# Stacks of q and k formed in place, one store per result of mixer A, and two more pairs of projection tiles by seven half products

## The chip, the cores and the metric

The kernel runs on one core of a Trainium2 chip, in one launch. The metric is the device time of that launch in microseconds (us); lower is better. TensorE (PE) multiplies matrices, VectorE (DVE) and ScalarE (ACT) do elementwise work and move results out of PSUM, GpSimd (POOL) and SyncE (SP) issue DMAs, and POOL also does small copies. Each engine carries out its own instructions in the order in which they stand in the program and waits for the others by semaphores.

## The reference, cut to what matters

One encoder layer for 512 tokens of width 1024, in float32. Two token mixers run beside each other on projections of the input `h`, are gated and merged, and a SwiGLU block follows.

```python
qa, ka, va, qb, kb, vb = jnp.split(h @ w_in, SPLITS, axis=-1)      # 16, 4, 4, 12, 12, 12 heads of 64
qa, ka, qb, kb = (rope_partial(t, pos) for t in (qa, ka, qb, kb))  # rotates the first 16 of 64
o_a = windowed_gqa_sink(qa, ka, va, a_sink)     # |i-j| <= 128, 4 query heads per key head
o_b = dilated_mixture(qb, kb, vb)               # (window, stride) = (128,1), (512,4), (2048,16)
g_a, g_b = jnp.split(jax.nn.sigmoid(h @ w_gate + b_gate), 2, axis=-1)
y = (g_a * (o_a @ w_br_a) + g_b * (o_b @ w_br_b)) @ w_out
h = layer_norm(DN_ALPHA * h + y, ln1_g, ln1_b)
f = (silu(h @ w_ff_gate) * (h @ w_ff_up)) @ w_ff_down
h = layer_norm(DN_ALPHA * h + f, ln2_g, ln2_b)
```

## The kernel before, in words

**Numbers.** Each float32 operand of a matmul is split into a rounded high part and a low part (what the rounding left), and a product is three matmuls: high by high, high by low, low by high. ACT (sometimes DVE) makes the high part, DVE the low part by a subtraction. For attention, high and low parts stand as a *stack* of 128 partitions: for a query head the 64 rows of its high part above the 64 rows of its low part, for a key head the high part twice (`t`) and the low part twice (`kl`), or, for the dilated groups, pairs of high and low columns, twice (`k_pairs`). `q_post`, `k_post` and `k_pairs` form them after the rotation: one copy and one subtraction give the parts of both heads of a tile, and SP's DMAs (`move`, L821; in `k_pairs` L866) put 64 rows at a time in their places.

**Projection tiles.** A tile of 128 output features is a sum over eight blocks of 128 inputs: 24 matmuls of 512 columns (`feat_k`, L533 to L535). Two tiles together can also be formed by `pair_x` (L649 to L651) as a 2 by 2 block product with seven instead of eight half products, 12 matmuls of 256 columns each, so 84 in all. It loads five half-tile weights and adds two more onto them by accumulating DMAs of POOL (L397), forms two sums on DVE, and splits seven half tiles instead of four. ACT and DVE put the results together.

**Attention.** Mixer A has four groups of heads (words `A0` to `A3`), each in four blocks of 128 queries. Mixer B has four head slots (`B0` to `B3`). In B, a block's statistics are exchanged between partition blocks by POOL's small copies (L1128, L1129) ahead of the normalisation. The outputs of A leave in DRAM tiles `oa`, two stores of 64 partitions per block (L1056). Later `fetch_oa` (words `O`) loads two heads as 128 rows (SP, L1317) and adds their other part by an accumulating DMA of POOL (L1318).

**Order.** `ORDER` lists the work in words: `P:x,y` a pair by `pair_x`, `T:x`, `Q..`, `K..` a single tile, `q`, `g`, `V..` further single tiles, `R` the rotation of the tiles gathered so far, `A`, `B`, `O` as above. A planner at build time (`Program.run`) gives each operation a due time from the PE work ahead of it and then fixes the order of every engine by costs that stand in the code. It also hands out the SBUF slots. Raw weight halves are limited by `ws` (`N_WS` = 6), split ones by `whl` (`N_WHL` = 12, two slots per half), later somewhat more (`ROOMS`). After the mixers come the branch products, `w_out`, the feed-forward block (also with seven half products) and the last layer norm; the change edits nothing there.

Of the kernel before, what the change touches and what calls it, by code (L numbers as in the profile page):

```python
# [9 lines left out]
F32 = mybir.dt.float32  # L10
# [5 lines left out]
P = 128  # L16
# [36 lines left out]
SPARE, SPARE2 = 12, 12  # L53
# [12 lines left out]
RATE, RATE2, ACC = 1.4, 1.3, 290  # L66

# [19 lines left out]
VA q1 A0 q2 q3 g X P:k1,q4 R A1 P:q5,g P:q6,q7 R A2 P:g,g A3 P:g,g L P:Q00,K00 R V12 P:Q01,K01 R P:Q02,K02 R V0 B0 Q10 K10 R Q11 K11 R B1 O O Q12 K12 R O O B2 B3 O O O O g8  # L87
"""
FORMS = -60.0
VAL = -100.0  # L90
OA_AFTER = (0, 0, 0, 0, 0, 0, 0, 0)
# [3 lines left out]
BY_DMA = ()  # L95
AWAY = range(8, 16)
N_WSA, N_WHLA = 8, 16
# [36 lines left out]
class Program:  # L134
# [68 lines left out]
    def run(self):  # L203
# [27 lines left out]
        while n_left:  # L231
# [13 lines left out]
            while progress:  # L245
                progress = False
                for e in engines:
# [31 lines left out]
                    if e == SP:  # L279
                        end = now + (0.62 if 14 < now < SLOW else 0.47)  # L280
                        moved = max(moved, now + 0.9) + (1.5 if now < 9.5 else RATE if 90 < now < 165 else RATE2 if 285 < now < 325 else 1.0 if now < SLOW else 0.92) * cost
                        o.done = moved + (LATE if 95 < now < 150 else 2.4 if 14 < now < SLOW else 0.87)
                    elif o.moves:
                        end = now + cost
                        moved = max(moved, end + 0.3) + (1.0 if 14 < now < SLOW else 0.92) * o.moves
                        o.done = moved + (0.87 if e == ACT else 6.2 if ACC < now < 420 else 3.2 if 14 < now < SLOW else 2.2)
                    else:
                        end = now + cost
                        o.done = end
# [51 lines left out]
def hybrid_layer(ctx: ExitStack, tc: tile.TileContext, wpack, xT, xtok, sink, bgate,  # L341
# [262 lines left out]
    def pair_x(ua, ub):  # L604
# [12 lines left out]
        def form(key, of, x, y):  # L617
            tt(lambda: W[of].t, lambda: W[x].t, lambda: W[y].t, ALU.add, [W[x], W[y]], [W[of]], S, -LOOK)
            W[key] = W[of]
# [92 lines left out]
    def turn_rows(tiles):  # L712
# [12 lines left out]
        op([(DVE, dve(S, extra=0.03))], lambda e: nc.vector.stream_shuffle(h_(), g(), SHUF2), reads=gs, writes=[H], prio=EV)  # L725
        op([(DVE, dve(S))], lambda e: nc.vector.tensor_tensor(g(), g(), c.t[0:n], op=ALU.mult),
           reads=[*gs, *[(c, i) for i in range(4)]], writes=gs, prio=EV)
        op([(DVE, dve(S))], lambda e: nc.vector.tensor_tensor(h_(), h_(), s_.t[0:n], op=ALU.mult),
           reads=[H, *[(s_, i) for i in range(4)]], writes=[H], prio=EV)
# [78 lines left out]
    def both_parts(ps, nt):  # L808

        R = rotate(ps)  # L810
        x, y = slot(F32R), slot(F32R)
        op(cp_alts(S, cut=CUT), lambda e: copy(e, view(x.t, nt, False), view(R.t, nt, True)),
           reads=[R], writes=[x, (y, "room")], prio=EV)
        op([(DVE, dve(S, extra=CUT))], lambda e: nc.vector.tensor_tensor(
            view(y.t, nt, False), view(R.t, nt, True), view(f32(x.t), nt, False), op=ALU.subtract),
           reads=[R, x], writes=[y], prio=EV)
        return x, y

    def move(dst, d, src, c, key, rooms=()):

        op([(SP, 0.4)], lambda e: nc.sync.dma_start(f32(dst.t[d:d + 64]), f32(src.t[c:c + 64])), reads=[src],  # L821
           writes=[(dst, key), *rooms], prio=EV)

    def q_post(ps, nt, kv_half):

        x, y = both_parts(ps, nt)
        out_ = []
        for a in (0, 64):
            t = slot(F32R)
            move(t, a, x, a, "h", [(t, "room")])  # L830
            move(t, 64 - a, y, a, "l")
            out_.append((t, a))
        return out_

    def k_post(ps, nt):

        x, y = both_parts(ps, nt)
        out_ = []
        for a in (0, 64):
            t, kl = slot(F32R), slot(F32R)  # L840
            for b, src in ((t, x), (kl, y)):
                for d, key in ((a, "h"), (64 - a, "d")):
                    move(b, d, src, a, key, [(kl, "room" + key)] if b is t else [])
            out_.append((t, kl))
        return out_

    def k_pairs(ps):

        R = rotate(ps)
        zs, out_ = [], []  # L850
        for n in range(2):
            z, c = slot(F32R), slice(n * (S // 2), (n + 1) * (S // 2))
            zs.append(z)
# [7 lines left out]
        for a in (0, 64):  # L861
            ts = []
            for z in zs:
                t = slot(F32R)
                for d, key in ((a, "h"), (64 - a, "d")):
                    op([(SP, 0.4)], lambda e, t=t, z=z, a=a, d=d: nc.sync.dma_start(  # L866
                        f32(t.t[d:d + 64]), f32(z.t[a:a + 64])), reads=[(z, "h"), (z, "l")],
                       writes=[(t, key)] + ([(t, "room")] if key == "h" else []), prio=EV)
                ts.append(t)
            out_.append(tuple(ts))  # L870
        return out_
# [14 lines left out]
    def turned_values(u, nt, turn_by=0, done=None):  # L886
# [3 lines left out]
        for i in range(2):  # L890
            ps = done
# [18 lines left out]
        for b in range(NR):  # L910
# [6 lines left out]
            op([(PE, 0.18)], turn, reads=[*src, ident], writes=[pb])  # L917
# [59 lines left out]
    def turned_probs(srcs, toks):  # L977
# [7 lines left out]
        op([(PE, 0.36)], go, reads=[*toks, ident], writes=[pb])  # L985
# [6 lines left out]
    def turned_pairs(srcs, toks):  # L992
# [7 lines left out]
        op([(PE, 0.36)], go, reads=[*toks, ident], writes=[pb])  # L1000
# [12 lines left out]
    oaD = [Buf("dram", None, lambda: dram.tile([2, 4, 64, 4, P], F32, name=name("oa"))) for _ in range(4)]  # L1013
    obT = [slot(F32, "res") for _ in range(2)]

    def unit_a(g, b, qs, kk, vs):
# [38 lines left out]
        for part in range(2):  # L1055
            op([(SP, 0.73)], lambda e, part=part: nc.sync.dma_start(  # L1056
                oaD[g].t[part, :, :, b].rearrange("h p c -> p h c"),
                t.t[64 * part:64 * part + 64].rearrange("p (h c) -> p h c", h=4)), reads=[t], writes=[(oaD[g], b, part)],
               prio=STORE)

    def unit_b(hs, q, k, v0, v1, v2):
# [99 lines left out]
        dil = []  # L1161
        for half in range(2):
# [5 lines left out]
            def pv(e, half=half, xs=xs, od=od):  # L1168
# [7 lines left out]
                y for vs in (v1, v2) for t in vs[2 * half:2 * half + 2] for y in vtok(t)], writes=[od])  # L1176
            t = slot(F32, "att")
            dil.append(t)
            part = lambda od=od: od.t.rearrange("p (r i a) -> p r a i", r=2, a=2)
# [32 lines left out]
        t = slot(F32, "att")  # L1212
        op(cp_alts(S, True), lambda e: copy(e, t.t[0:64], o.t[64:128]), reads=[o], writes=[t])
        a = 64 * (hs % 2)
# [27 lines left out]
    def gate(f, ps=None):  # L1242
        if ps is None:
# [6 lines left out]
           reads=[ps, bg], writes=[t], prio=EV)  # L1250

# [25 lines left out]
    ka = k_near(psk, 4)  # L1277
    qa = q_near(psq, 4, (0, 0))
# [32 lines left out]
    def fetch_oa(k):  # L1311
# [3 lines left out]
        src = lambda part: d.t[part, hs].rearrange("h p b c -> (h p) (b c)")  # L1315
        got = [(d, b, part) for b in range(NR) for part in range(2)]
# [5 lines left out]
    def units_of(w):  # L1322
# [8 lines left out]
        if w[0] == "q":  # L1331
            return U_QA + i, lambda t: qa.extend(q_post(t, 4, ((i // 2) % 2,) * 2))
        if w[0] == "k":
            return U_KA + i, lambda t: ka.extend(k_post(t, 4))
# [4 lines left out]
    def step(w):  # L1339
# [4 lines left out]
        elif w[:2] == "P:":  # L1344
            both = [units_of(x) for x in w[2:].split(",")]
            for (u, f), t in zip(both, pair_x(*[u for u, _ in both])):
# [7 lines left out]
        elif w == "R":  # L1354
            tiles = [t for t, _ in env["turn"]]
            turn_rows(tiles)
# [8 lines left out]
        elif w[0] == "q":  # L1365
            i = int(w[1])
            kv = (i // 2) % 2
            qa.extend(dense_q(U_QA + i, 4, (kv, kv)))
        elif w == "k1":
            ka.extend(dense_k(U_KA + 1, 4))  # L1370
        elif w[0] == "A":
            g = int(w[1])
            for b in range(NR):
                unit_a(g, b, qa[4 * g:4 * g + 4], ka[g], env["va"])
# [4 lines left out]
        elif w[0] in "QK":  # L1379
            pair, g = int(w[1]), int(w[2])  # L1380
            u, f = units_of(w)
            env["turn"].append((in_sbuf(u), f))
        elif w == "V0":
# [11 lines left out]
    for w in ORDER.split():  # L1395
        step(w)

# [167 lines left out]
    def turn_h1(t, j, c0, c1, tok):  # L1565
# [7 lines left out]
        op([(PE, 0.36)], go, reads=[z, ident], writes=[pb], prio=NORM)  # L1573
# [482 lines left out]
```

## Time and profile before

| | |
|---|---|
| median of 3 runs | 727.33 us (727.32 to 727.66) |
| the profiled execution | 727.14 us, its span 725.4 us |
| busy | PE 716.7 us (99%), DVE 655.7 (90%), ACT 472.0 (65%), POOL 133.1 (18%) |
| DMA | 140.30 MB, mean 193 GB/s |

The span runs from the first to the last instruction. Matmuls overlap in their pipeline, so the duration of one matmul is longer than the time from its start to the next one's; the cost of a matmul in a row of matmuls is read from starts.

### The profile page before, as it was taken

The numbers are of one execution on the slowest core, as the hardware profiler recorded it, in microseconds if no ns is written. First come the engines' busy times: TensorE is split into PE (matmuls) and PEld (weight loads), VectorE is DVE, ScalarE is ACT, GpSimd is POOL, SyncE is SP. The second block draws the span as 40 slices with busy tenths as digits, with TensorE's granted clock in tenths as the row PEclk, the third lists the DMA queues.
The fourth block names the chain that finished last, engine by engine and source line by source line (L and its number), as shares of the span: only waits on it lengthen the run. The fifth ranks groups of instructions, "written<-read, shape, count | busy, mean of one in ns | idle before, by whom it ended". The sixth has DMA issues, their size and how long they took to land.

```text
span 725.4 us, 14382 instructions
## 1 busy us (share of the span) xinstructions
PE 716.7 (99%) x4767; PEld 665.7 (92%) x4767; DVE 655.7 (90%) x1408; ACT 472.0 (65%) x1077; POOL 133.1 (18%) x297
## 2 busy tenths in 40 slices
PE   9999999999999999999999999999999999999995
PEld 7889999989998888988888999999999999999985
DVE  6999999889997898898968898899999999899987
ACT  6757798768778665766624666756666566666821
POOL 0021221101100731540020022111112111212000
PEclk9999999999999999999999999999999999999999
DMA  7978788856567699965782499676788878978402
GB/s 250 320 154 199 193 221 245 211 130 173 168 190 188 158 239 249 317 203 163 232 189 71 102 273 239 154 202 148 196 256 215 194 193 246 248 194 195 103 30 87
DMA packets 88010, 140.30 MB, mean 193 GB/s; under 512 B 11136, under 2 KB 24064, under 8 KB 87936
## 3 DMA queue, kind: packets, MB, share of 16 engines
q1 hardware_dynamic: 74336, 114.87, 51.2%
q0 software_dynamic: 13328, 24.39, 20.5%
q8 instruction: 37, 0.61, 0.3%
q14 instruction: 37, 0.30, 0.1%
q10 hardware_dynamic: 272, 0.13, 0.1%
HBM read 114.97 MB, written 7.60 MB: 169 GB/s over the span
## 4 chain that ended last, share of the span: by engine, by line
PE 98%; DMA 1%; DVE 1%; ACT 0%; DVEq 0%; SPq 0%; issue 0%
PE ps L1702 10%; PE ps L1701 9%; PE ps L1700 9%; PE ps L534 9%; PE ps L533 9%; PE ps L535 9%; PE ps L1911 4%; PE ps L1913 4%; PE ps L1912 4%; PE ps L651 3%; PE ps L650 3%; PE ps L649 3%; PE ps L983 3%; PE ps L1491 3%; PE ps L1492 3%; PE ps L1490 3%
## 5 line engine op out<-in xcount | busy, mean ns | idle before, releaser
L383 ACT ACTIVATE sl<-sl 128x512 fp32r<-128x512 f32 (+3 forms) x419 | 231.3, 583 | 58.9 <-DVE sl L554 31.0
L554 DVE TENSOR_TENSOR sl<-sl,sl 128x512 fp32r<-128x512 f32 (+3 forms) x378 | 222.8, 623 | 4.4 <-ACT sl L383 3.4
L383 ACT ACTIVATE sl<-ps 128x256 f32<-128x256 f32 (+5 forms) x209 | 88.5, 445 | 90.9 <-PE ps L1702 56.2
L397 POOL DMA_DIRECT2D sl<-wpack x60 | 53.0, 887 | 341.5 <-DMA sl<-wpack 130.2
L1701 PE MATMUL ps<-sl,sl 128*128 128x256 f32 x352 | 96.8, 275 | 0.0
L1702 PE MATMUL ps<-sl,sl 128*128 128x256 f32 x352 | 96.8, 275 | 0.0
L1700 PE MATMUL ps<-sl,sl 128*128 128x256 f32 x352 | 96.8, 275 | 0.0
L533 PE MATMUL ps<-x,sl 128*128 128x512 f32 (+1 forms) x241 | 93.4, 388 | 0.0
L535 PE MATMUL ps<-x,sl 128*128 128x512 f32 (+1 forms) x241 | 91.3, 379 | 0.0
L534 PE MATMUL ps<-x,sl 128*128 128x512 f32 (+1 forms) x209 | 79.2, 379 | 0.1
L1700 PE MATMUL ps<-x,sl 128*128 128x256 f32 x264 | 72.6, 275 | 0.0
L1701 PE MATMUL ps<-x,sl 128*128 128x256 f32 x264 | 72.6, 275 | 0.0
L1702 PE MATMUL ps<-x,sl 128*128 128x256 f32 x264 | 72.6, 275 | 0.0
L1701 PEld LDWEIGHTS ps<-sl,sl 128*128 128x128 f32 x352 | 67.6, 192 | 0.1
L1700 PEld LDWEIGHTS ps<-sl,sl 128*128 128x128 f32 x352 | 67.6, 192 | 0.1
L1702 PEld LDWEIGHTS ps<-sl,sl 128*128 128x128 f32 x352 | 67.6, 192 | 0.0
L409 DVE TENSOR_TENSOR sl<-sl,sl 128x512 fp32r<-128x512 f32 x94 | 62.9, 683 | 0.8 <-ACT sl L383 0.7
L535 PEld LDWEIGHTS ps<-x,sl 128*128 128x128 f32 x241 | 45.7, 190 | 6.4
L1700 PEld LDWEIGHTS ps<-x,sl 128*128 128x128 f32 x264 | 50.6, 192 | 0.4
L1701 PEld LDWEIGHTS ps<-x,sl 128*128 128x128 f32 x264 | 50.6, 192 | 0.4
L533 PEld LDWEIGHTS ps<-x,sl 128*128 128x128 f32 x241 | 45.8, 190 | 5.6 <-ACT x L383 0.4
L554 DVE TENSOR_TENSOR sl<-sl,ps 128x512 f32<-128x512 f32 (+1 forms) x67 | 44.1, 660 | 7.4 <-PE ps L1913 5.4
(172 smaller groups left out, 1856.9 us busy)
## 6 DMA issues: line engine op xcount, KB each, us to landing
sl<-wpack SPq DMA_DIRECT2D x249, 256.0 KB, 4.0
sl<-wpack POOLq DMA_DIRECT2D x60, 256.0 KB, 5.4
sl<-sl SPq DMA_DIRECT2D x110, 128.0 KB, 3.3
wf<-wpack SPq DMA_DIRECT2D x51, 256.0 KB, 5.4
wf<-wpack POOLq DMA_DIRECT2D x24, 256.0 KB, 5.4
oa<-sl SPq DMA_DIRECT2D x32, 128.0 KB, 3.3
sl<-sl SPq DMA_DIRECT2D x68, 32.0 KB, 2.6
sl<-oa SPq DMA_DIRECT2D x8, 256.0 KB, 4.7
```

Of the source, the lines that this page charges most:

```text
L383: nc.scalar.activation(dst, src, AF.Copy)
L397: op([(POOL, 1.0)], lambda e: nc.gpsimd.dma_start(b.t, src2, accum_op=ALU.add), reads=[b], writes=[b], prio=prio, moves=1.65)
L409: op([(DVE, dve(S))], lambda e: nc.vector.tensor_tensor(l.t, src.t, f32(h.t), op=ALU.subtract), reads=[src, h], writes=[l], prio=prio, abs ...
L533: mm(o, a, x0, start=(k == 0 and begins), stop=False, skip_group_check=split)
L534: mm(o, a, x1, start=False, stop=False, skip_group_check=split)
L535: mm(o, b, x0, start=False, stop=(k == nk - 1), skip_group_check=split)
L554: op([(DVE, dve(w))], lambda e: nc.vector.tensor_tensor(dst(), x(), y(), op=o), reads=reads, writes=writes, prio=prio)
L1700: mm(o, wh, pairs(bh[k]()), start=(first and k == 0), stop=False, skip_group_check=True)
L1701: mm(o, wh, pairs(bl[k]()), start=False, stop=False, skip_group_check=True)
L1702: mm(o, wl, pairs(bh[k]()), start=False, stop=(k == 3), skip_group_check=True)
L1911: mm(ps.t, x0, pairs(w[0].t), start=(first and m == 0), stop=False, skip_group_check=True)
L1912: mm(ps.t, x0, pairs(w[1].t), start=False, stop=False, skip_group_check=True)
```

## The change

Three things are edited, and the planner's constants and the word list with them.

1. `q_post` copies the rounded parts into both stacks at full height, and one move for each head puts the low part over the half that the head doesn't need. `k_post` and `k_pairs` do the same: full copies on ACT, then moves of 64 rows within the tile. A query tile takes 2 moves instead of 4, a key tile 4 instead of 8. Each move now also waits for those who still read the half that it overwrites.
2. The DRAM tiles `oa` are laid out head by head, then part, so a block of mixer A leaves by one store of 128 partitions. A fetch of two heads then reads two runs of 64 rows that don't adjoin, instead of one run of 128 rows.
3. The word list has ten `P:` words instead of eight (`Q10` and `K11`, and one more pair of gates), in another order, and each word may carry a shift of its due time (`@`). All gates with f >= 8 are put away in DRAM and fetched back, three more than before.

```diff
-VA q1 A0 q2 q3 g X P:k1,q4 R A1 P:q5,g P:q6,q7 R A2 P:g,g A3 P:g,g L P:Q00,K00 R V12 P:Q01,K01 R P:Q02,K02 R V0 B0 Q10 K10 R Q11 K11 R B1 O O Q12 K12 R O O B2 B3 O O O O g8
+X@2 g@-35 q1@-105 q2@-149 T:q3@-22 VA@-123 P:k1,q4@-23 R@-465 A0@-87 P:Q00,g@-38 A1@-79 P:q6,q7@-7 P:g,g@-8 R@-25 P:g,g A3@-83 L@-49
+P:q5,K00@-17 R@2 V12@-14 A2 P:Q01,K01@-52 R@-13 P:Q02,K02@-16 R@-62 V0@-6 Q11@-75 P:K11,Q10@-8 R@16 K10@-18 R@-1160 B0@-95 Q12@-15 K12@-37
+g@-17 B1@-63 R@-429 O@-43 O@93 O@-87 B2@-368 g@6 B3@20 O@-46 O@182 O@-16 P:g,g@-4 g@-28 g@2 g O@66 O@85 g@-6
...
     def q_post(ps, nt, kv_half):
-        x, y = both_parts(ps, nt)
-        out_ = []
-        for a in (0, 64):
-            t = slot(F32R)
-            move(t, a, x, a, "h", [(t, "room")])
-            move(t, 64 - a, y, a, "l")
-            out_.append((t, a))
-        return out_
+        R = rotate(ps)
+        q0, q1, l = slot(F32R), slot(F32R), slot(F32R)
+        rounded(R, q0, nt, [(l, "room")])
+        low_of(R, q0, l, nt)
+        move(q0, 64, l, 0, "l", [(q0, "h"), (l, "h")])
+        rounded(R, q1, nt, by_act=True)
+        move(q1, 0, l, 64, "l", [(q1, "h"), (l, "h")])
+        return [(q0, 0), (q1, 64)]
+    def spread(t, u, reads):
+        op(cp_alts(S)[:1], lambda e: copy(e, u.t, f32(t.t)), reads=reads, writes=[(u, "h"), (u, "room")], prio=EV)
     def k_post(ps, nt):
...
+        R = rotate(ps)
+        t0, l0, t1, l1 = [slot(F32R) for _ in range(4)]
+        rounded(R, t0, nt, [(l0, "room")])
+        low_of(R, t0, l0, nt)
+        move(t0, 64, t0, 0, "d", [(t0, "h"), (l0, "h")])
+        rounded(R, t1, nt, [(l1, "room")], True)
+        spread(l0, l1, [(l0, "h")])
+        move(l0, 64, l0, 0, "d", [(l0, "h"), (l1, "h")])
+        move(t1, 0, t1, 64, "d", [(t1, "h")])
+        move(l1, 0, l1, 64, "d", [(l1, "h")])
...
-    oaD = [Buf("dram", None, lambda: dram.tile([2, 4, 64, 4, P], F32, name=name("oa"))) for _ in range(4)]
+    oaD = [Buf("dram", None, lambda: dram.tile([4, 2, 64, 4, P], F32, name=name("oa"))) for _ in range(4)]
...
-        for part in range(2):
-            op([(SP, 0.73)], lambda e, part=part: nc.sync.dma_start(
-                oaD[g].t[part, :, :, b].rearrange("h p c -> p h c"),
-                t.t[64 * part:64 * part + 64].rearrange("p (h c) -> p h c", h=4)), reads=[t], writes=[(oaD[g], b, part)],
-               prio=STORE)
+        op([(SP, 1.46)], lambda e: nc.sync.dma_start(
+            oaD[g].t[:, :, :, b].rearrange("h a p c -> (a p) h c"), t.t.rearrange("p (h c) -> p h c", h=4)),
+           reads=[t], writes=[(oaD[g], b)], prio=STORE)
...
-        src = lambda part: d.t[part, hs].rearrange("h p b c -> (h p) (b c)")
+        src = lambda part: d.t[hs, part].rearrange("h p b c -> h p (b c)")
         op([(SP, 0.73)], lambda e: nc.sync.dma_start(st.t, src(0)), reads=got, writes=[st], prio=OAP[k // 4], after=env["B", OA_AFTER[k]])
         op([(POOL, 1.0)], lambda e: nc.gpsimd.dma_start(st.t, src(1), accum_op=ALU.add), reads=[*got, st], writes=[st],
            prio=OAP[2 + k // 4], moves=1.65)
...
     def gate(f, ps=None):
...
+        if f in AWAY:
+            put_away(f)
...
+LONG = 1.3
```

Three places of the program show what moved; line numbers are those of each kernel's own file.

PE before, at the single tile of `Q10` in the middle of the mixers (`x` are the tokens' high and low parts, `ident` marks a transpose):

```order
L1049 MATMUL ps_3155<-sl_3143,sl_566 128x512
L1050 MATMUL ps_3155<-sl_3144,sl_566 128x512
L533 MATMUL ps_3171<-x_94,sl_2909 128x512
L534 MATMUL ps_3171<-x_103,sl_2909 128x512
L535 MATMUL ps_3171<-x_94,sl_2910 128x512
L915 MATMUL ps_3179<-ident,sl_3045 128x128
```

PE after, where the pair of `K11` and `Q10` begins:

```order
L1018 MATMUL ps_3368<-ident,sl_3179 128x128
L1018 MATMUL ps_3368<-ident,sl_3182 128x128
L659 MATMUL ps_3375<-x_98,sl_3189 128x256
L660 MATMUL ps_3375<-x_105,sl_3189 128x256
L661 MATMUL ps_3375<-x_98,sl_3190 128x256
```

Triples of 512 columns have become triples of 256: over the whole program there are 96 matmuls of 128x512 fewer and 168 of 128x256 more; all others are as many as before, and there is one run of transposes less (50 instead of 51).

SP before, at the first fetches of `oa` (L391 are weights, L722 and L733 rows of the rotation):

```order
L391 DMA sl_3871<-wpack 128x512
L722 DMA sl_3840<-sl_3853 16x512
L1317 DMA sl_3903<-oa_1071 128x512
L1317 DMA sl_3915<-oa_1071 128x512
L391 DMA sl_3921<-wpack 128x512
L733 DMA sl_3573<-sl_3582 16x512 x2
L733 DMA sl_3648<-sl_3582 16x512 x2
L1317 DMA sl_3979<-oa_2048 128x512
L391 DMA sl_3989<-wpack 128x512
```

SP after, at the same place (L842 are the moves within a stack):

```order
L395 DMA sl_3764<-wpack 128x512
L754 DMA sl_3601<-sl_3607 16x512 x2
L732 DMA sl_3507<-sl_3812 16x512 x2
L1369 DMA sl_3846<-oa_1974 128x1x512
L1369 DMA sl_3855<-oa_1021 128x1x512
L1369 DMA sl_3861<-oa_1974 128x1x512
L1369 DMA sl_3877<-oa_3163 128x1x512
L395 DMA sl_3880<-wpack 128x512
L395 DMA sl_3931<-wpack 128x512
L842 DMA sl_3923<-sl_3923 64x512
L842 DMA sl_3919<-sl_3919 64x512
```

Four fetches stand in a row, three more and one follow 21 and 45 rows later; their shape has become one of two runs; SP has 528 transfers instead of 586, 54 moves and 16 stores fewer.

POOL before, behind the copies of a unit of mixer B:

```order
L1128 COPY st_3646<-st_3646 32x2
L1129 COPY st_3646<-st_3646 32x2
L1318 DMA sl_3903<-oa_1071 128x512
L1318 DMA sl_3915<-oa_1071 128x512
L1318 DMA sl_3979<-oa_2048 128x512
L1318 DMA sl_3996<-oa_2048 128x512
L1318 DMA sl_4186<-oa_2534 128x512
```

POOL after, within the copies of a unit of mixer B (`B1`):

```order
L1162 COPY st_3660<-st_3660 32x2
L1370 DMA sl_3846<-oa_1974 128x1x512
L1370 DMA sl_3855<-oa_1021 128x1x512
L1370 DMA sl_3861<-oa_1974 128x1x512
L1370 DMA sl_3877<-oa_3163 128x1x512
L1161 COPY st_3660<-st_3660 32x2
L1162 COPY st_3660<-st_3660 32x2
```

Four accumulating fetches now stand ahead of the last eight copies of `B1`; before they stood behind the last copy.

More of the change, by code (lines that the diff above doesn't have):

```diff
@@ L819, in move, with low_of @@
[L819 to L824, printed above, removed]
-        x, y = both_parts(ps, nt)
-        out_ = []
-        for a in (0, 64):
-            t = slot(F32R)
-            move(t, a, x, a, "h", [(t, "room")])
-            move(t, 64 - a, y, a, "l")
-            out_.append((t, a))
-        return out_
-    def k_post(ps, nt):
[L837 to L845, printed above, removed]
+    def low_of(R, h, l, nt):
+        op([(DVE, dve(S, extra=CUT))], lambda e: nc.vector.tensor_tensor(
+            view(l.t, nt, False), view(R.t, nt, True), view(f32(h.t), nt, False), op=ALU.subtract),
+           reads=[R, (h, "h")], writes=[(l, "h")], prio=EV)
@@ L860, in k_pairs @@
                prio=EV)
[L861 to L871, printed above, removed]
+            zs.append(z)
+        for z in zs:
+            u = slot(F32R)
+            spread(z, u, [(z, "h"), (z, "l")])
+            us.append(u)
+            move(z, 64, z, 0, "d", [(z, "h"), (z, "l"), (u, "h")])
+            move(u, 0, u, 64, "d", [(u, "h")])
+        return [tuple(zs), tuple(us)]
     def scores(o_of, q, qc, k, kc, n):
```

129 lines of the change are left out of this document (89 added, 40 removed).

## The prediction, as it stood before the changed kernel ran

> **What bounds the kernel now.** I read the page first, then TensorE's own waits, then its starts in the timeline, then the stretch of the mixers, where the change lies.
>
> ```profile
> span 725.4 us, 14382 instructions
> ...
> PE 716.7 (99%) x4767; PEld 665.7 (92%) x4767; DVE 655.7 (90%) x1408; ACT 472.0 (65%) x1077; POOL 133.1 (18%) x297
> ...
> PE 98%; DMA 1%; DVE 1%; ACT 0%; DVEq 0%; SPq 0%; issue 0%
> ```
>
> The second line is busy time and share, the last the chain that ended last. A busy TensorE may still wait inside its pipeline, so its waits (waited for: us in total, times, longest) and its end come next:
>
> ```profile
> PE ps L469 <- DVE eps L520: 1.2, 1, 1.2
> ```
>
> ```profile
> 717.62 0.38 PE L1492 MATMUL ps<-sl,sl 128*128 128x512 f32 x1
> 718.04 0.70 DVE L1529 BATCH_NORM_STATS2 st<-ps 128x6 f32<-128x512 f32 x1 [0.68 <-PE ps L1492]
> ...
> 720.53 1.54 DVE L1553 SCALAR_TENSOR_TENSOR sl<-sl,st,sl 128x512 f32<-128x512 f32 x3
> ```
>
> TensorE waits once, 1.2 us at the start. Its last matmul begins at 717.6, and 7.4 us of layer norm and output follow up to 725.4. In the order PE's first 169 and last 1,470 matmuls stand as before, so start and tail are kept. The kernel is a chain of matmuls: what leaves TensorE leaves the time, and anything else counts only once TensorE must wait for it.
>
> The cost of a matmul in the chain, from starts (start, duration, engine, line); 197 rows stand from first to last in the first piece, 104 in the second:
>
> ```profile
> 424.80 0.28 PE L1702 MATMUL ps<-sl,sl 128*128 128x256 f32 x1
> ...
> 446.58 0.28 PE L1702 MATMUL ps<-x,sl 128*128 128x256 f32 x1
> 446.69 0.28 PE L1700 MATMUL ps<-sl,sl 128*128 128x256 f32 x1
> ```
>
> ```profile
> 349.70 0.38 PE L533 MATMUL ps<-x,sl 128*128 128x512 f32 x1
> ...
> 371.93 0.38 PE L1491 MATMUL ps<-sl,sl 128*128 128x512 f32 x1
> ```
>
> (446.69 - 424.80) / 196 = 0.1117 us for 256 columns, (371.93 - 349.70) / 103 = 0.2158 us for 512. Two halves cost 0.0076 more than one whole.
>
> **The change part by part.**
>
> *Two more pairs.* A pair is 84 matmuls of 256 columns instead of 48 of 512: 84 x 0.1117 = 9.38 us for 48 x 0.2158 = 10.36. The word list has ten pairs instead of eight, and the order bears it out: 168 matmuls of 256 come, 96 of 512 go. 168 x 0.1117 - 96 x 0.2158 = 18.77 - 20.72 = **-1.95 us**, all on the path. One run of transposes less ends in a matmul; what that saves is in these rows:
>
> ```profile
> 70.17 1.04 PE L983 MATMUL ps<-ident,sl 128*128 128x128 f32 x8
> 70.96 0.36 PE L649 MATMUL ps<-x,sl 128*128 128x256 f32 x1
> 71.15 0.28 PE L650 MATMUL ps<-x,sl 128*128 128x256 f32 x1
> ```
>
> The matmul behind transposes takes 0.19 to the next start instead of 0.11: -0.08 us. Together **-2.03 us**. [...]
>
> *The pairs' other work.* Their splits and sums fall on DVE and ACT:
>
> ```profile
> L383 ACT ACTIVATE sl<-sl 128x512 fp32r<-128x512 f32 (+3 forms) x419 | 231.3, 583 | 58.9 <-DVE sl L554 31.0
> ...
> L554 DVE TENSOR_TENSOR sl<-sl,sl 128x512 fp32r<-128x512 f32 (+3 forms) x378 | 222.8, 623 | 4.4 <-ACT sl L383 3.4
> ...
> L409 DVE TENSOR_TENSOR sl<-sl,sl 128x512 fp32r<-128x512 f32 x94 | 62.9, 683 | 0.8 <-ACT sl L383 0.7
> ...
> L554 DVE TENSOR_TENSOR sl<-sl,ps 128x512 f32<-128x512 f32 (+1 forms) x67 | 44.1, 660 | 7.4 <-PE ps L1913 5.4
> ```
>
> ```profile
> core 0: us, PE busy (x) PEld busy (x) DVE busy (x) ACT busy (x) POOL busy (x), PEclk, DMA share, GB/s
> 20.00:60.00 40.00, 40.00 (x196) 35.16 (x195) 39.51 (x82) 23.79 (x47) 5.76 (x12) 1.00 0.81 224
> ...
> 260.00:300.00 40.00, 40.00 (x223) 35.88 (x221) 34.90 (x94) 24.19 (x60) 8.88 (x17) 1.00 0.99 250
> ...
> 20.00:345.00 325.00, 325.00 (x2057) 299.34 (x2056) 295.88 (x726) 239.76 (x585) 73.22 (x224) 1.00 0.76 206
> ```
>
> Two single tiles cost DVE four subtractions (4 x 0.683 = 2.7 us). A pair costs seven, two sums, and two steps to put it together, at most 9 x 0.683 + 2 x 0.660 = 7.5. That is 4.8 a pair, 9.5 for both. In the mixers (20 to 345) DVE is busy 295.9 of 325 us; 305.4 of 323 would be 95%. It stays below TensorE, and neither added pair lies in the full stretch at 20 to 60. I cost it at nothing; without that cover it would be up to 9.5 us. ACT, with 27 more copies of 128x512 in the order (27 x 0.583 = 15.7 us) and 85 us idle there, has room.
>
> *Stacks in place.* 54 moves leave SP.
>
> ```profile
> L821 SPq DMA_DIRECT2D sl<-sl x76: 461/564/1474, 50.5 to 283.1; - x76
> ...
> DMA to landing us min/median/max: 2.2/3.1/7.4
> ```
>
> ```profile
> SPq L821 <- ACT sl L383: 16.5, 6, 9.0
> ```
>
> 54 x 0.564 = 30 us of SP's issue, none of it on the path. Each remaining move now waits for a full copy and for the reader of the half it overwrites, about two ACT copies more (1.2 us). Behind it on SP stand weights. Before, moves held SP up to 9.0 us for ACT, and TensorE didn't wait; so 1.2 us is covered, and I cost it at nothing (bounds 0 and 1.2 us for each of the six rotation groups of mixer B, if a move decided).
>
> *Gates put away.* Three more stores and three more fetches of 256 KB, in a stretch where the branch products run; together 1.5 MB of some 140; they free three slots from then on. TensorE's next branch product is the only one that could wait for a fetch, and it is due long after. Nothing.
>
> *Stores and fetches of oa.* A block's output leaves by one store instead of two; nobody on the path waits for it. The fetches move the same bytes but read two runs of 64 rows:
>
> ```profile
> q1 hardware_dynamic: 74336, 114.87, 51.2%
> q0 software_dynamic: 13328, 24.39, 20.5%
> ...
> q10 hardware_dynamic: 272, 0.13, 0.1%
> ```
>
> ```profile
> sl<-wpack SPq DMA_DIRECT2D x249, 256.0 KB, 4.0
> ...
> sl<-oa SPq DMA_DIRECT2D x8, 256.0 KB, 4.7
> sl<-oa POOLq DMA_DIRECT2D x8, 256.0 KB, 7.0
> ...
> sl<-xT ACTq DMA_DIRECT2D x1, 128.0 KB, 2.5
> ```
>
> Issue to landing is 4.7 us on SP and 7.0 on POOL, and the order leaves tens of us to the first branch product. If a fetch lands as before, this too costs nothing. That is the condition on which the forecast stands.
>
> **Sum.** Span 725.4 - 2.03 = 723.3 us; 1.7 us lie around the span in the profiled execution (727.14 - 725.4). The median of the runs, 727.33, is 0.2 above that execution, so I predict 727.33 - 2.03 = **725.3 us**. Its own range is 724.9 to 726.0: the first microseconds, where ACT and DVE take some pieces in another order, are worth some 0.3 us either way, and a few hand-offs may cost 0.08 us each.
>
> **The rivals.** About 0.2% (1.45 us) is what a measurement of this kernel can tell from no change: faster ends at 725.9, slower begins at 728.8.
>
> *A: the fetches of oa crowd two DMA engines (slower).* Place: SP's four fetches in a row with weights behind them, then three, then one. Mechanism: a transfer is dealt out by the outer count of its access patterns. The one transfer of queue q10 left 272 packets, 256 pieces of 512 bytes and 16 more, one for each engine. All transfers of before can be dealt to 16 engines (their rows are 16, 32, 64 or 128). A source of two runs offers only two shares. Then 64 rows of 2 KB fall on each of two engines instead of 8 on each of 16. On q1 a byte costs 0.512 x 16 x 725.4 us / 114.87 MB, so 2 KB cost 106 ns; on q0 (0.205) they cost 200. A fetch on SP then holds two engines 64 x 0.106 = 6.8 us instead of 0.85, eight of them 47.6 us more, and every weight has its share on these engines too. The cover is the weights' lead: 6 raw and 6 split half tiles (`ws`, `whl`), at 12 x 0.2158 = 2.59 us of TensorE each, 31.1 us. So TensorE waits 47.6 - 31.1 = 16.5 us: 725.3 + 16.5 = **741.8**. It turns slower once the extra load passes 31.1 + 2.0 + 1.45 = 34.6 us. Bounds: 0 if the lead grows or the fetches spread in time, 47.6 if nothing hides; I take the middle since the eight lie close, where before shows the engines 0.99 busy (260 to 300). POOL adds to it: its four accumulating fetches wait for SP's, and the last eight copies of `B1` stand behind them, up to 4 x 6.8 = 27 us late. For it: nothing in before shows a transfer of so small an outer count going fast. Against it: nothing shows one going slowly either, and eight transfers are few. [...]
>
> *B: hand-offs of the mixers too tight (no change).* In the order the products of B's dilated part now follow their transposes after the work of at least 20 matmuls of 256 columns instead of 25, so 5 x 0.1117 = 0.56 us less for a copy and a subtraction. If four such places lose it, the gain of 2.03 shrinks by 2.2: **727.5**. For it: DVE at 95%. Against it: one wait in the whole of before.
>
> **How the numbers follow.** The forecast gets 0.50 (0.48 faster, 0.02 within), A 0.40 (0.38 slower, 0.02 within), B 0.10 (0.08 within, 0.02 slower). A has a high share because the pattern is new to this trace and the cover is finite. So 0.48 faster, 0.12 within 0.2%, 0.4 slower. The likeliest is 725.3. The range must reach into A: 725.0 to 745, which leaves out the fast end of the forecast and the dear third of A, some 0.18.
>
> **What would show it.** Right: TensorE's waits stay near 1.2 us, its last matmul begins near 715.6, the fetches of oa land in 4 to 8 us. For A: they land in 10 us or more, the 4-byte markers of q1 fall short, and the weights behind them (L395) become what TensorE waits for near 255 to 310. For B: short waits on DVE (L989 to L1044 of the new file) between 230 and 340. Wrong altogether: a wait elsewhere, or DVE at 99% through the mixers.

## The result, and the profile after

The changed kernel takes 788.28 us (median of 4 runs, 787.44 to 789.21), the kernel before 727.50 beside it: a ratio of 1.0835, 95% interval 1.0816 to 1.0854. The forecast was 725.3 us with a range up to 745.0, so the sign and the size are both wrong. The profiled execution has a span of 785.6 us, 60.2 more than before.

The page of the changed kernel: busy times, then the span in 40 slices of 19.6 us (tenths busy, granted clock, DMA), then the chain that ended last.

```profile
span 785.6 us, 14514 instructions
...
PE 726.4 (92%) x4839; PEld 672.9 (86%) x4839; DVE 665.8 (85%) x1431; ACT 483.9 (62%) x1103; POOL 142.9 (18%) x301
...
PE   9999999999999818384999999999999999999996
...
PEclk9999999999999957697999999999999999999998
...
PE 77%; DMA 15%; DVE 3%; SPq 3%; issue 1%; ACT 1%; DVEq 0%; POOLq 0%; ACTq 0%
PE ps L1758 9%; PE ps L1759 9%; PE ps L1757 9%; DMA sl<-oa 7%; DMA sl<-wpack 4%; PE ps L537 4%; PE ps L538 4%; PE ps L539 4%; PE ps L659 4%; PE ps L661 4%; PE ps L660 4%; PE ps L1968 3%; PE ps L1969 3%; PE ps L1970 3%; PE ps L1018 3%; DMA sl<-sl 3%
```

Before, the chain was 98% TensorE and every slice full. Now the loss lies in one place, slices 14 to 19 (255 to 373 us), the granted clock falls there too, and the fetches of `oa` hold 7% of the chain: 55 us. TensorE's waits in the changed kernel (total, times, longest):

```profile
PE ps L537 <- ACT sl L387: 14.6, 1, 14.6
PE ps L1018 <- ACT sl L1006: 14.4, 3, 11.5
PE ps L1250 <- DVE sl L1023: 12.4, 1, 12.4
PE ps L659 <- ACT sl L667: 5.1, 2, 4.2
PE ps L903 <- DMA sl<-sl: 2.2, 1, 2.2
```

The large ones come singly and long, and name ACT and DVE, not a DMA. One step behind each of them stands another wait. ACT's waits for DMAs of `oa` and of weights between 255 and 365 us, and the ACT timeline around the longest (start, duration, and in brackets the idle time before it):

```profile
ACT sl L387 <- DMA sl<-oa: 31.0, 3, 16.8
ACT sl L387 <- DMA sl<-wpack: 9.1, 2, 5.0
```

```profile
268.31 1.27 ACT L387 ACTIVATE sl<-ps 128x256 fp32r<-128x256 f32 x3
286.41 1.15 ACT L387 ACTIVATE sl<-sl 128x512 fp32r<-128x512 f32 x2 [16.82 <-DMA sl<-oa]
```

The copy that splits a fetched tile stands at the head of ACT's queue and waits 16.8 us for the fetch; TensorE's wait of 14.6 for rounded weights (L537) is for a copy that stands behind it. POOL's fetches (L1370), and the same line of the kernel before (L1318) behind it:

```profile
L1370 POOL DMA_DIRECT2D sl<-oa x8: 1344/1347/1376, 265.0 to 349.5; - x8
...
  DMA sl<-oa: 51.6, 3
...
DMA to landing us min/median/max: 16.0/17.8/22.1
```

```profile
DMA to landing us min/median/max: 4.3/7.0/8.9
```

A fetch that landed after 7.0 us now lands after 17.8, and POOL stood 51.6 us waiting for SyncE's halves before it could issue three of them. How two engines look in a table by stretch, first the kernel before, then after (the last two columns are the share of the 16 DMA engines and GB/s):

```profile
255.00:275.00 20.00, 20.00 (x113) 17.90 (x112) 17.86 (x45) 14.00 (x31) 5.45 (x7) 1.00 0.96 236
275.00:300.00 25.00, 25.00 (x142) 22.46 (x141) 21.74 (x59) 13.36 (x36) 5.43 (x13) 1.00 0.98 268
```

```profile
255.00:275.00 20.00, 17.97 (x122) 16.58 (x120) 15.51 (x38) 11.67 (x28) 11.99 (x22) 1.00 0.21 47
275.00:300.00 25.00, 8.15 (x31) 6.75 (x32) 4.78 (x14) 3.96 (x9) 4.09 (x10) 0.52 0.57 132
```

From 0.96 of the engines to 0.21, while SyncE's fetches are under way (issued from 255.8 us on): most of the engines have nothing to do. The queues of the changed kernel say which transfers:

```profile
q1 hardware_dynamic: 70928, 110.02, 44.9%
q0 software_dynamic: 21072, 25.49, 20.2%
```

By packet size, q1 holds 8,336 markers of 4 bytes: 520 transfers x 16 and 8 x 2 (before: 9,376, 586 x 16). The eight fetches of SyncE ran on two engines each. On q0, 7,168 packets of 8 bytes are new: 8 x 14 x 64, which by the count is one for each of 64 rows on each of the 14 engines that carry nothing of POOL's fetches.

### The profile page after: what moved, and what is told of

Read it like the earlier page. It is cut to its first block, busy times and chain, and to the rows that moved or that the text cites. A ratio compares the mean times of both kernels' runs of the same rounds, so it can differ in the third digit from the quotient of the medians.

```text
span 785.6 us, 14514 instructions
## 1 busy us (share of the span) xinstructions
PE 726.4 (92%) x4839; PEld 672.9 (86%) x4839; DVE 665.8 (85%) x1431; ACT 483.9 (62%) x1103; POOL 142.9 (18%) x301
## 4 chain that ended last, share of the span: by engine, by line
PE 77%; DMA 15%; DVE 3%; SPq 3%; issue 1%; ACT 1%; DVEq 0%; POOLq 0%; ACTq 0%
PE ps L1758 9%; PE ps L1759 9%; PE ps L1757 9%; DMA sl<-oa 7%; DMA sl<-wpack 4%; PE ps L537 4%; PE ps L538 4%; PE ps L539 4%; PE ps L659 4%; PE ps L661 4%; PE ps L660 4%; PE ps L1968 3%; PE ps L1969 3%; PE ps L1970 3%; PE ps L1018 3%; DMA sl<-sl 3%
## 5 line engine op out<-in xcount | busy, mean ns | idle before, releaser
L387 ACT ACTIVATE sl<-sl 128x512 fp32r<-128x512 f32 (+3 forms) x446 | 246.1, 586 | 101.6 <-DVE sl L558 37.9
L558 DVE TENSOR_TENSOR sl<-sl,sl 128x512 fp32r<-128x512 f32 (+3 forms) x396 | 234.0, 627 | 6.6 <-DMA sl<-wpack 3.3
L387 ACT ACTIVATE sl<-ps 128x256 f32<-128x256 f32 (+6 forms) x212 | 89.0, 441 | 73.8 <-PE ps L1759 52.7
L401 POOL DMA_DIRECT2D sl<-wpack x64 | 56.8, 888 | 362.5 <-DMA sl<-wpack 109.4
L537 PE MATMUL ps<-x,sl 128*128 128x512 f32 (+1 forms) x209 | 83.2, 398 | 14.6 <-ACT sl L387 14.6
L539 PE MATMUL ps<-x,sl 128*128 128x512 f32 (+1 forms) x209 | 81.4, 390 | 0.0
L538 PE MATMUL ps<-x,sl 128*128 128x512 f32 (+1 forms) x177 | 69.2, 391 | 0.1
L413 DVE TENSOR_TENSOR sl<-sl,sl 128x512 fp32r<-128x512 f32 x86 | 58.0, 685 | 1.1 <-ACT sl L387 0.7
L537 PEld LDWEIGHTS ps<-x,sl 128*128 128x128 f32 x209 | 41.2, 197 | 19.8 <-ACT sl L387 15.1
```

What stands on the lines that cost most here:

```text
L387: nc.scalar.activation(dst, src, AF.Copy)
L401: op([(POOL, 1.0)], lambda e: nc.gpsimd.dma_start(b.t, src2, accum_op=ALU.add), reads=[b], writes=[b], prio=prio, moves=1.65)
L413: op([(DVE, dve(S))], lambda e: nc.vector.tensor_tensor(l.t, src.t, f32(h.t), op=ALU.subtract), reads=[src, h], writes=[l], prio=prio, abs ...
L537: mm(o, a, x0, start=(k == 0 and begins), stop=False, skip_group_check=split)
L538: mm(o, a, x1, start=False, stop=False, skip_group_check=split)
L539: mm(o, b, x0, start=False, stop=(k == nk - 1), skip_group_check=split)
```

## The experiments

**One run again, or two runs alone.** Two kernels undo and redo the suspected part by itself. The first is the changed kernel with a fetch of one run; the same edit of `src` and of the tile, turned round, made the second out of the kernel before.

```diff
-dram.tile([4, 2, 64, 4, P], F32, name=name("oa"))
+dram.tile([2, 4, 64, 4, P], F32, name=name("oa"))
-        src = lambda part: d.t[hs, part].rearrange("h p b c -> h p (b c)")
+        src = lambda part: d.t[part, hs].rearrange("h p b c -> (h p) (b c)")
```

> The changed kernel with one thing undone: the mixer result's DRAM tile has the two parts outermost again, so each of its eight fetches reads one run of 128 rows; each result is stored by two stores, issued back to back where the one store stood. The order of the instructions on every engine is that of the changed kernel. Theory (fetches in two runs of 64 rows were dealt to two DMA engines, and all the lost time follows from that): the 61.7 us of waits and slow matmuls of TensorE go, 4-byte markers of the SyncE queue rise to 16 for every one of its DMAs, and the time is the forecast's 725.3 us, 724.5 to 727. Rival (the stacks formed in place and the new order bring tight hand-offs): it stays at 775 us or more.

> The kernel before with one thing changed: the mixer result's DRAM tile has the heads outermost, so the eight pairs of fetches read two runs of 64 rows; two stores for each result stay, and so do the order, the stacks and the pairs of before. Theory (two engines): most of the loss shows without any other part of the change, 745 to 790 us; SyncE's queue shows 8 x 14 markers of 4 bytes less than before, and the accumulating fetches leave 7168 packets of 8 bytes. Rival (stacks and order): 727.5 us, as before.

Measured: 729.83 us for the first (ratio to before 1.0030, 1.0017 to 1.0043), 787.6 for the second (1.0821, 1.0806 to 1.0837). The cost of fetches in two runs is shown from both sides: 58.5 of the 60.8 us go with it, and it alone, in the order and with the pairs and stacks of before, costs 60.1. So neither stacks nor pairs nor order are needed for the loss. The second kernel's packets show the same two engines: 112 markers fewer on q1 (8 x 14) and 7,168 packets of 8 bytes on q0. The first theory's second half fell: 729.8 is not 725.3. TensorE's waits in the first of the two:

```profile
PE ps L1139 <- DMA sl<-sl: 1.4, 1, 1.4
PE ps L473 <- DVE eps L524: 1.2, 1, 1.2
PE ps L659 <- ACT sl L667: 1.1, 2, 0.6
PE ps L1208 <- DVE sl L1043: 0.5, 1, 0.5
```

Four short waits, 3.0 us together, have come beside the one of before (L473 here). They are taken up below.

**Which queue.** SyncE's fetches, then GpSimd's, each as two transfers of one run of 64 rows, the other left in two runs.

```diff
-lambda e: nc.sync.dma_start(st.t, src(0))
+lambda e: [nc.sync.dma_start(st.t[64 * i:64 * i + 64], row(0, i)) for i in range(2)][-1]
```

> The changed kernel with SyncE's eight fetches issued as two DMAs of 64 rows each (one run each, at the same place in the queue); GpSimd's accumulating fetches stay in two runs. Theory A (SyncE's queue matters: the half units of weights stand behind its fetches): the wait of 14.8 us for weights near 272 us goes and with it what follows, about 740 us (735 to 755). Theory B (GpSimd's queue matters: the last copies of statistics stand behind its accumulating fetches, which land after 17.8 us each): 755 to 780 us, with the waits of 12.5 us at the window product (near 316 us) and 11.6 us at the transposes (near 359 us) left.

> The changed kernel with GpSimd's eight accumulating fetches issued as two DMAs of 64 rows each (one run each); SyncE's fetches stay in two runs. Theory A (SyncE's queue matters): 755 to 780 us, with the waits for weights near 272 us left. Theory B (GpSimd's queue matters): about 740 us (735 to 755), with the waits at the window product and the transposes gone.

Measured: 760.92 us (1.0461, 1.0430 to 1.0491) with GpSimd's fetches alone on two engines, 762.33 (1.0487, 1.0470 to 1.0503) with SyncE's alone. Both theories, that one queue matters and the other doesn't, fall: either half costs as much as the other, 31.1 and 32.5 us above the 729.83 with none, and they nearly add up (63.6 for 58.5). Their ways differ. With GpSimd's alone, ACT waits for the fetches themselves (which land after 21.2 us), and DVE for ACT:

```profile
ACT sl L387 <- DMA sl<-oa: 22.9, 4, 10.6
ACT x L387 <- DMA sl<-oa: 9.0, 1, 9.0
```

```profile
DVE sl L1355 <- ACT sl L387: 21.1, 3, 10.2
```

With SyncE's alone, ACT waits for weights that stand in SyncE's queue behind the fetches, and DVE for POOL's copies of statistics (which stand behind the wait for SyncE's half) and for a stack's move:

```profile
ACT sl L387 <- DMA sl<-wpack: 18.6, 2, 11.3
```

```profile
DVE st L1169 <- POOL st L1162: 17.9, 2, 13.8
DVE sl L1023 <- DMA sl<-sl: 15.4, 1, 15.4
```

The last of these ends at TensorE as 14.6 us at the window product; in the chain, the move of 128 KB took 12.3 us to land, where moves took a median of 3.1 (L821) and 4.8 (L866) before.

**How many engines.** Four runs of 32 rows instead of two of 64: the source's outer count is 4.

```diff
-dram.tile([4, 2, 64, 4, P], F32, name=name("oa"))
+dram.tile([4, 2, 2, 32, 4, P], F32, name=name("oa"))
-        src = lambda part: d.t[hs, part].rearrange("h p b c -> h p (b c)")
+        src = lambda part: d.t[hs, :, part].rearrange("h x p b c -> (h x) p (b c)")
```

> The changed kernel with the mixer result's tile cut so that each fetch reads four runs of 32 rows in place of two of 64 (and each result is stored by four stores of 32 partitions at the place of the one); order as in the changed kernel. Theory (a fetch's runs are dealt to as many engines as there are runs, and the cost is the time on those engines): four engines, with half the rows on each, the loss of 61 us falls to less than half, 740 to 757 us, and SyncE's queue shows markers of 12 engines missing at each of its 8 fetches. Rival (any fetch of more than one run is slow in itself): 780 us or more. Second rival (the cover of 31 us holds 8 x 32 rows x 106 ns = 27 us): 729 us.

Measured: 753.56 us (1.0360, 1.0336 to 1.0384).

```profile
q1 hardware_dynamic: 71712, 110.02, 46.6%
q0 software_dynamic: 16976, 25.46, 20.7%
```

q0 now holds 3,072 packets of 8 bytes, 8 x 12 x 32, and q1 9,120 markers, 568 x 16 and 8 x 4: four engines carry a fetch. POOL's land after a median of 12.8 us, between the 17.8 with two engines and the 7.3 with 16. Over the 729.8 us with 16 engines, the cost is 58.5 us with two and 23.7 with four (its four stores for one are in this too). That is 0.41 of it; the rows on an engine above the 8 of a full spread are 24 instead of 56, 0.43. The theory's range held, and the first rival (780 us or more) fell. The second rival fell too, and with it the idea that the weights' lead of 31 us is a cover that must first be used up.

**Whether the splits at the head of the queues do it.** GpSimd's fetches alone on two engines, and the planner told to expect them later, so the splits stand further back; beside it, the kernel with fetches on 16 engines and the same number, which has the same order of work on PE, ACT and DVE.

```diff
-6.2 if ACC < now < 420 else
+15 if o.moves == 1.6501 else 6.2 if ACC < now < 420 else
```

> The run with GpSimd's fetches alone on two engines, and one number more: the planner is told that such a fetch lands 15 us after it is issued, so the copies that split the fetched tile are queued 24 to 30 places later on ScalarE and 39 to 43 later on VectorE for the first three fetches. Theory (those 33 us were lost because the splits stood at the head of ScalarE's and VectorE's queues while the fetch landed, and the copies that TensorE needs stood behind them): the loss falls to less than half, 730 to 745 us, and ScalarE's waits for the fetched tile between 255 and 365 us fall from 31.9 us to under 12. Rival (GpSimd's packets on two engines hold up the weights and moves on those engines): 755 us or more again.

> As the run before it, with 15 us in place of 10. Theory (hand-offs that the order decides): 725.5 to 729 us, best case the forecast's 725.3 us, if no wait over 0.3 us is left between 255 and 365 us. Rival (no slack): 729.5 us or more.

> The run with fetches of one run and two stores (729.8 us), and the planner told that an accumulating fetch lands 10 us after its issue, so the copies that split the fetched tile stand some 20 places later on ScalarE and VectorE. Theory (its waits of 0.8 us at the half products near 272 us and of 2.2 us near 289 to 293 us are hand-offs that the order decides): the first goes, the second may stay: 726 to 729 us. Rival (the order of the changed kernel has no slack anywhere, and a shift brings other waits): 729.5 us or more.

Measured: 751.5 us (1.0326, 1.0306 to 1.0347) for the first, 740.2 (1.0170, 1.0154 to 1.0185) for the second, 739.55 (1.0166, 1.0150 to 1.0181) for the third. The first came out between its theory's range and its rival's: the new order costs 10.4 us by itself. Read against the second, two engines cost 11.3 us in this order, with the splits early 31.1. ACT's waits for the fetch in the first fell from 31.9 us to 2.7, although they land hardly sooner (a median of 20.0 us for 21.2):

```profile
ACT x L387 <- DMA sl<-oa: 1.6, 1, 1.6
...
ACT sl L387 <- DMA sl<-oa: 1.1, 1, 1.1
```

So the block at the head of ACT's and DVE's queues is a large part of GpSimd's 31 us: 9.4 of them went outright (760.92 to 751.5), and 19.8 if the whole cost of the new order is taken off. The second figure is an upper one, since the waits that the new order has anyway can hide part of a late landing. For SyncE's 32 us no such test was made; there the waits above are what is known. As attempts at a better order both late versions failed: TensorE then waits 5.3 us (with 15 us) and 4.2 us (with 10) at L537 between 311 and 319 us. Their theory fell; the rival (no slack) is what was measured.

**Where the gain of 2 us went.** The fetches in one run of 64 rows twice, with the one store kept; then the kernel with one run of 128 rows without the moves of the stacks.

> The changed kernel with its one store for each mixer result, but each of the 16 fetches (SyncE's and GpSimd's) issued as two DMAs of one run of 64 rows; order as in the changed kernel. Theory (the run before this one, with one run of 128 rows and two stores, kept 4.0 us of waits, which come from the tight hand-offs of the new order): again 728 to 731 us, with waits of some tenths of a us to 2 us near 66 and between 272 and 293 us. Rival (those waits come from the two stores or from that layout): 725 to 726 us, the forecast.

> The kernel with fetches of one run and two stores, and with the moves by DMA that complete the stacks of q and k left out at their places (54 DMAs of 128 KB; half of each stack then holds other numbers); copies and order stay. Theory A (the four waits of 3.6 us are for these moves and for transfers behind them): 726 to 727 us, no wait at the scores near 292 us. Theory B (the waits are those of the pairs and of the order, whatever the moves do): 729 to 730 us.

Measured: 730.77 us (1.0049, 1.0036 to 1.0063), so it isn't the stores. This run also settles a rival for the large loss: the rows lie in DRAM as in the changed kernel, two runs that don't adjoin, and still the 58 us are gone. It is the number of runs in one transfer that costs, not where they lie. And 727.49 without moves (1.0000, 0.9989 to 1.0011), so the moves cost 2.3 us there, nearer to theory A. Between 260 and 300 us no wait was left, but one of 1.0 us at the half products near 66 us was. The time is still 2.2 us over the forecast, and apart from this wait no cause was found for that. The stacks and the pairs alone, in the kernel before:

```diff
-... V0 B0 Q10 K10 R Q11 K11 R B1 O O Q12 K12 R O O B2 B3 O O O O g8
+... V0 B0 P:Q10,K10 R Q11 K11 R B1 O O Q12 K12 R O O B2 B3 O O O O P:g,g g6
```

> The kernel before with the stacks of q and k formed in place by half as many moves, and nothing else of the change (pairs, stores, fetches and the list that sets the order as before; the planner lays the instructions anew). Theory (the forecast's term: the moves in place cost nothing by themselves): 727.4 us, 726.5 to 728.5. Rival (the copies that now wait for a move's two halves make TensorE wait wherever they are not given room by the order): 730 us or more, with waits at transposes of probabilities or scores of mixer units.

> The kernel before with two more pairs of projection tiles by half products, and nothing else of the change: Q10 with K10, and two of the last eight gate tiles. Theory (a pair takes 0.97 us from TensorE and everything else stays covered): 727.5 - 1.95 = 725.6 us. Rival (with pairs come waits for their halves' copies, as between 66 and 272 us in the run with fetches of one run): 727 us or more, with waits at the half products.

Measured: 728.31 us for the stacks (1.0005, 0.9996 to 1.0014): no difference. 734.91 for the two pairs (1.0104, 1.0089 to 1.0118). Since a pair's sum is -0.97 us, each was then tried by itself, and over the stacks.

> The kernel before with one more pair by half products, Q10 with K10, and nothing else of the change. Theory (the 4.8 us of waits between 200 and 220 us in the run with both pairs are this pair's: its tiles are due within the mixer's units): 731 to 733 us. Rival (those waits come only with both pairs): 727.5 - 0.97 = 726.5 us.

> The kernel before with one more pair by half products, two of the last eight gate tiles, and nothing else. Theory (a pair pays where its tiles are due late and waits of about 2 us near 320 us and 0.9 us near 412 us are all it adds): 728 to 730 us. Rival (it is covered): 727.5 - 0.97 = 726.5 us.

> The kernel before with the stacks formed in place and with both more pairs (Q10 with K10, two of the last gates), stores and fetches as before. Theory (hand-offs as with the pairs alone, the stacks add nothing): 733 to 737 us. Rival (half as many moves leave the queue room and the pairs' halves come in time): 725.5 to 728 us.

> The kernel before with the stacks formed in place and one more pair, two of the last gate tiles. Theory: as the gates' pair alone, 728 to 730 us. Rival (covered): 726.5 us, a version that beats both kernels.

Measured: 733.89 us (1.0079, 1.0065 to 1.0093), 733.88 (1.0085, 1.0071 to 1.0099), 744.27 (1.0232, 1.0211 to 1.0254) and 732.0 (1.0064, 1.0051 to 1.0077). In the second and third a part of the output came out changed without any part being left out, for a reason that was not found, so nothing rests on those two. The time of both pairs is the rival's (727 us or more), but only 0.7 us of its waits stand at the half products. The pair of `Q10` and `K10` missed its 731 to 733 us by 0.9, and the gates' pair over the stacks its 728 to 730 by 2.0. The pair of `Q10` and `K10` doesn't pay by itself. TensorE's longer waits with it alone, then the stretch of 205 to 225 us in the kernel before, with the pair alone, and with the stacks alone:

```profile
PE ps L983 <- ACT sl L971: 1.2, 2, 1.0
PE ps L1571 <- DVE sl L1553: 0.8, 1, 0.8
PE ps L1050 <- DVE sl L988: 0.8, 2, 0.7
PE ps L649 <- DVE st L1032: 0.7, 1, 0.7
```

```profile
205.00:225.00 20.00, 20.00 (x115) 17.88 (x114) 17.04 (x47) 16.86 (x43) 1.17 (x7) 1.00 0.72 192
205.00:225.00 20.00, 16.72 (x102) 14.36 (x101) 18.37 (x51) 16.05 (x43) 1.91 (x8) 0.93 0.63 163
205.00:225.00 20.00, 20.00 (x110) 17.94 (x109) 18.09 (x49) 14.46 (x36) 1.39 (x4) 1.00 0.60 176
```

DVE is busy 18.4 of 20 us there (17.0 before), and TensorE's short waits name DVE and ACT in turn. But DVE's load alone doesn't explain them: with the stacks alone it is busy 18.1 of 20 us and TensorE is full. The chain of the run with the pair goes through SyncE's queue there: from 203.2 to 208.8 us eight moves (L866) and a weight are issued one behind the other, ahead of a transfer that DVE waits for.

```profile
207.51 0.60 SPq L866
...
208.79 2.15 DMA sl<-sl
210.94 0.69 DVE sl L988
```

Adding a pair also makes the planner lay the whole order anew. Which of these the 6.2 us come from isn't shown. No version was found that beats both kernels: the kernel before, and the same with stacks in place, are level and the fastest of all that do the whole work.

## Why the prediction was wrong, point by point

- **What bounds the kernel: right.** Nearly all that was lost is seen as TensorE's waits and as matmuls at a lower clock.
- **Stores and fetches of `oa`: wrong, and this is the step that failed.** It read "If a fetch lands as before, this too costs nothing. That is the condition on which the forecast stands." The condition doesn't hold: SyncE's fetches are dealt to two engines (8 x 2 markers), POOL's land in 17.8 us instead of 7.0, and this part alone costs 58.5 to 60.1 us.
- **Rival A: right in mechanism, mis-sized.** It gave 741.8 us. Its two engines stood (the markers fell short, weights came late), but not its sign that TensorE would wait for weights: between 255 and 365 us ACT waits 9.1 us for weights and 31.0 for `oa`. Its cover was the mistake: 47.6 us of load against 31.1 of the weights' lead, 16.5 left. With four engines the same sum is 8 x (3.4 - 0.85) = 20.4 against 31.1, no wait at all, and 23.7 us were measured. The lead covers only who waits through weights. It doesn't cover the splits of `oa` at the head of ACT's and DVE's queues, the copies of statistics behind POOL's fetches, or a move behind SyncE's. And the sum had one half of the load only: POOL's fetches, costed there as something that "adds to it", are worth 31.1 us of their own. The prediction had their price, 200 ns for a row of 2 KB on q0, which is 12.8 us for 64 rows, and used it nowhere; 17.8 us to land were measured.
- **What a wait costs beyond itself** was in no term. The waits of the changed kernel sum to 50.1 us beside the one of before, and the span is 60.2 longer though about 2 us of matmuls are gone: some 12 us are left. Most of them are the clock, below: in the stretches for which the profile gives half the clock, 56 matmuls took 8.7 us more than the usual steps of their shapes.
- **How many engines carry a fetch: right, and given too little weight.** The markers of q1 show 16 engines for each of the 586 transfers of before (9,376), two for a fetch with an outer count of 2 (8 x 2 of 8,336) and four with 4 (8 x 4 of 9,120). When the prediction was made no run showed two engines; they stood there as A's mechanism, and A got less (0.40) than the forecast (0.50). Nothing in the trace spoke for the forecast on this point either: no transfer of so small an outer count was seen going fast. A hope that nothing in the trace supported should not have had the larger share.
- **Two more pairs, -1.95 us: right for TensorE's own work, not seen in the time.** With each matmul at the median step of its shape, TensorE's work is 716.3 us before and 714.4 with the two pairs more. The step "I cost it at nothing", for what the pairs put on the other engines, failed: one pair alone makes the kernel before 6.2 us slower, with 4.0 us of new waits for DVE and ACT. Its reason was DVE's share of the time, 95% through the mixers, which says nothing of single hand-offs; whether DVE's work, SyncE's queue or the order laid anew makes them late stays open. In the order of the changed kernel less is lost: with fetches on 16 engines 2.3 us over before instead of 2.0 under it, 4.3 in all, and the next point takes 2.3 of these.
- **Stacks in place, nothing: right by themselves** (1.0005). In the changed kernel's order the moves that are left cost 2.3 us (729.83 to 727.49 without them), inside the bounds given (0 to 7.2).
- **Rival B** named the right kind of cost, hand-offs, had it too small (2.2 us expected, 2.0 + 2.3 = 4.3 with fetches on 16 engines) and mostly with another giver: of the 3.0 us of waits only 0.5 (L1208, for DVE) is what it described; the others are for a move (L1139) and for ACT at half products (L659).
- **Gates put away, nothing:** no wait of TensorE names them; not tried apart.

## What to carry to other kernels

Read the outer count of the source's access pattern whenever a DMA's layout changes: 2 instead of 128 in these fetches left the bytes alike and cost 58.5 to 60.1 us. The question of cover must be asked for each queue that a late transfer stands in, not for one: a copy that waited 16.8 us at the head of ACT's queue held up those behind it, and TensorE waited 14.6 us for one of these, whatever lead the weights had. And where TensorE is full and DVE near it, a saving on TensorE isn't a saving until those that must feed it faster, DMA queues included, are shown to have room in that stretch: the pair of `Q10` and `K10` took 0.97 us of matmuls away and made the kernel before 6.2 us slower.

## What the runs showed of the hardware

In the changed kernel the granted clock fell to half in each of the three longest waits of TensorE and came back only 3.4 to 5.6 us after TensorE had started again: it was 0.50 from 275.2 to 299.1 us (waits of 14.6 and 4.2 us, over at 287.6 and 293.5), from 319.6 to 333.2 (a wait of 12.4, over at 329.0) and from 364.0 to 374.2 (a wait of 11.5, over at 370.8). It was 0.50 from 305.9 to 309.3 as well, while TensorE worked, behind waits of 1.1 and 1.8 us. TensorE's timeline of the changed kernel after its waits of 14.6 and 4.2 us:

```profile
288.62 0.63 PE L539 MATMUL ps<-x,sl 128*128 128x512 f32 x1
293.50 0.58 PE L659 MATMUL ps<-sl,sl 128*128 128x256 f32 x1 [4.24 <-ACT sl L667]
...
297.93 0.63 PE L538 MATMUL ps<-x,sl 128*128 128x512 f32 x1
298.36 0.63 PE L539 MATMUL ps<-x,sl 128*128 128x512 f32 x1
298.78 0.42 PE L659 MATMUL ps<-x,sl 128*128 128x256 f32 x1
```

From 293.50 to 298.78 stand 12 matmuls of 256 columns and 6 of 512: 5.28 us for what takes 12 x 0.1117 + 6 x 0.2158 = 2.64 otherwise. Steps of 512 columns are 0.43 us (298.36 - 297.93) instead of 0.2158. So the steps behind these two waits cost another 2.6 us after the waits were over, and they were still long 5.3 us after the second start.

The packets of 8 bytes were not expected either: by their counts, an accumulating fetch of GpSimd left one for every row of an engine's share on each engine that it didn't use (7,168 with two engines, 3,072 with four, none with 16). SyncE's queue holds no such packet in the changed kernel nor with four engines, only fewer markers.
